# Conformer convolution accumulated in two PSUM banks, and 40 modulation row sums split between GpSimd and ScalarE

## The chip, the cores and the metric

The kernel runs on one core of a Trainium2 chip. The metric is the time of one execution on the device, in microseconds (us); lower is better. The engines are TensorE (PE, matmuls and transposes; PEld is its weight load), VectorE (DVE), ScalarE (ACT), GpSimd (POOL) and SyncE (SP, which issues most DMA transfers). Each engine works through its own queue of instructions strictly in order, and an instruction whose inputs or buffers are not ready holds up everything behind it in that queue.

## The reference

One layer of a hybrid diffusion backbone: 1024 latent tokens of width 1024 (16 rows of 64), and a prefix of 256 context tokens. All arithmetic is fp32. Cut to what matters here:

```
mx = split(silu(c) @ w_ada + b_ada, 6);  mc = split(silu(c_ctx) @ w_ada + b_ada, 6)
hx = modulate(rms_norm(x),   mx[0], mx[1])        # latent tokens
hc = modulate(rms_norm(ctx), mc[0], mc[1])        # context tokens
kc, vc, gtc = project_state_inputs(hc, w_in)      # the context gives keys, values, gates
fin_c       = mlstm_bidir_final(kc, vc, gtc)
ax, glx, qx, kx, vx, ox, gtx = project(hx, w_in)
hm = mlstm_bidir(qx, kx, vx, gtx, fin_c)          # 4 heads, chunked, both directions
u  = silu(layer_norm(dwconv31(ax * sigmoid(glx))))   # width 31 along rows of 64, 512 channels
y  = concat(u, sigmoid(ox) * head_norm(hm)) @ w_out
x  = x + mx[2] * rms_norm(y)
x  = x + mx[5] * rms_norm(conv_ffn(modulate(rms_norm(x), mx[3], mx[4])))
```

## The kernel before, in words

Channels lie on the 128 partitions, tokens along the free dimension. A matmul operand is split into a high and a low half (`hi` by a rounding copy on ScalarE, `lo = x - hi` by a subtraction on VectorE or GpSimd), and each product is three matmuls: hi·hi, hi·lo, lo·hi.

Stages, in order of time. (1) Norm and modulation of the latent tokens, and the first half of the gated projection for channel blocks j = 0 and 1. (2) `glu_evac` (L271) takes the two PSUM tiles of one block and one half of the tokens: sigmoid on ScalarE, product on VectorE (L274), which gives `u[j]`, a tile of 128 channels x 1024 tokens. Blocks j = 2 and 3 follow, one projection each. (3) `vpass(1)` multiplies ten token tiles by the value and gate weights of two heads (L556 to L558): eight latent tiles first, then two context tiles; ScalarE copies the values out (L562), VectorE the gate columns (L565). Ahead of the sixth tile the code calls `ctx_prepare`, which norms and transposes the context, scales it (L358, VectorE) and splits it into `hcT`: hi on ScalarE (L362), lo on VectorE (L363). The last two tiles of `vpass(1)` read `hcT`, so they need L362 and L363. (4) `gates` (L574 to L657), a chain of small VectorE operations and PE transposes, which needs the gate columns of all ten tiles. `vpass(0)`, the values of the other two heads, and the key and query projections run about it. (5) The four mLSTM heads; their denominators are chains of tiny VectorE operations on a tile `dn` (L813 to L818). (6) Output projection, from 460.9 us, then the FFN to the end.

Beside this runs the depthwise convolution, `conv(j)` for each of the 4 channel blocks (L276). ScalarE starts an accumulator with the middle tap and the bias (L278), and 30 `scalar_tensor_tensor` instructions on VectorE (L286, "taps") add the other taps, one after another and in place: accumulator = u shifted x weight + accumulator, over 784 to 1008 elements. The accumulator `accf` lies in two SBUF tiles of the pool `s8`, one for j = 0 and 1, one for j = 2 and 3. `hcT` takes two later tiles of the same pool. The convolutions stand in `prio(100000)`: the framework's scheduler, which fixes one order per engine when the program is built, puts such an instruction where nothing more urgent is ready by its own reckoning. The result is only read by `conv_norm`, late in the heads.

The modulation vectors `c @ w_ada` are row sums on VectorE: `mod_sum` (L228) multiplies a 128 x 1024 tile of the weights by the broadcast vector and accumulates each row's sum into one column, in one instruction. The first ones belong to stage 1. `ada_stream` issues 48 later ones: 16 for the context (`w` = 1, tiles `t`), ahead of the convolutions, and 32 for the latent tokens (`w` = 0, tiles `raw`), spread over stages 4 and 5.

GpSimd makes `lo` halves of some weights (L134, L382), a few memsets, and the small power operations of the norms (L141).

PSUM has eight banks of 512 fp32 columns: pool `mm` holds four tiles of one bank, pool `tp` four. `TP()` gives the next tile of `tp`. In the heads each chunk takes two of them, `pv` and `pc`.

Of the kernel before, what the change touches and what calls it, by code (L numbers as in the profile page):

```python
# [8 lines left out]
F32 = mybir.dt.float32  # L9
F32R = mybir.dt.float32r  # L10
AF = mybir.ActivationFunctionType
ALU = mybir.AluOpType

P = 128
# [10 lines left out]
CW = 31  # L25
W = 64
# [4 lines left out]
def hybrid_block(ctx: ExitStack, tc: tile.TileContext, x, cx, cc, small, gb, w_ada,  # L31
                 wblk, wva, wvb, w_out, w_up, w_down, out):
    nc = tc.nc
    act, dve, pool, pe, sp = nc.scalar, nc.vector, nc.gpsimd, nc.tensor, nc.sync
# [7 lines left out]
    wp = wide.enter_context(tc.tile_pool(name="wp", bufs=11))  # L42
    s8 = wide.enter_context(tc.tile_pool(name="s8", bufs=12))
    mm = wide.enter_context(tc.tile_pool(name="mm", bufs=4, space=bass.MemoryType.PSUM))
    tp = wide.enter_context(tc.tile_pool(name="tp", bufs=4, space=bass.MemoryType.PSUM))
    early = ExitStack()
    t4 = early.enter_context(tc.tile_pool(name="t4", bufs=10))

# [20 lines left out]
    def wide_tile(n, per, dt=F32):  # L69

        return Cols([S8(dt).rearrange("p (k n) -> p k n", k=per) for _ in range(n // per)])
# [10 lines left out]
    def MM():  # L82
        return mm.tile([P, 512], F32, tag="mm", name="mm")

    def TP():
        return tp.tile([P, 512], F32, tag="tp", name="tp")

    def H2(n=512):
        return sm.tile([P, 512], F32, tag="h2", name="h2", bufs=8)[:, 0:n]
# [137 lines left out]
    def mod_sum(r, s, w, ch, k):  # L227
        dve.scalar_tensor_tensor(out=r, in0=r, scalar=1.0, in1=s, op0=ALU.mult, op1=ALU.mult,  # L228
                                 accum_out=mod[:, w, ch, k:k + 1])
# [45 lines left out]

    def conv(j):  # L276
        uv = u[j].rearrange("p (r c) -> p r c", c=W)
        act.activation(out=accf[:, j], in_=u[j], func=AF.Identity, scale=conv_w[:, j, 15:16],  # L278
                       bias=conv_b[:, j:j + 1])
        for t in range(CW):  # L280
            o = t - 15
            if o == 0:
                continue
            lo, hi = max(0, -o), min(W, W - o)
            dst = accf[:, j].rearrange("p (r c) -> p r c", c=W)[:, :, lo:hi]
            dve.scalar_tensor_tensor(out=dst, in0=uv[:, :, lo + o:hi + o], scalar=conv_w[:, j, t:t + 1],  # L286
                                     in1=dst, op0=ALU.mult, op1=ALU.add)


    AB2 = const.tile([P, 2, 8], F32, name="AB2")  # L290
    Gt = {}

    def ada_stream(jobs, pl):
        for w, ch, done in jobs:
            s = ada_rows(w)
            for k in range(KT):
                r = pl()
                sp.dma_start(r, w_ada[ch * KT + k])
                mod_sum(r, s, w, ch, k)
                if done and k == KT - 1:  # L300
                    done()
                yield
# [173 lines left out]
    for j in range(2):  # L476
        u[j] = T4()
        for hf in range(2):
            glu_evac(j, hf, *ps0[j, hf])
    accf = wide_tile(4, 2)  # L480
    vw = None
    with prio(100000):
        conv(0)
# [260 lines left out]
    def mlstm_head(h):  # L744
# [38 lines left out]
        for g in range(2):  # L783
# [9 lines left out]
            for t in range(4):  # L793
                if t == 2 and pend and hn is not None:
                    yield from tails()
                c = 4 * g + t
                cs = slice(c * P, (c + 1) * P)
                pv, pc = TP(), TP()
                nv = pv[:, 0:258].rearrange("p (d n) -> p d n", d=2)
                nc_ = pc[:, 0:258].rearrange("p (d n) -> p d n", d=2)  # L800
                pl.matmul(pc[:, 0:258], qT[:, cs], Cs[c // 4][:, c % 4].rearrange("p d n -> p (d n)"),
                          start=True, stop=True)
                yield
                for d in range(2):
                    pl.matmul(nv[:, d], Dt[d][:, cs], vx[h][:, c, :], start=True, stop=True)
                    yield
                gc = gcol(0, h, c)
                gs = slice(gc, gc + 63, 62)

                dn = SM(4, "dn")  # L810
                rr, rw = dn[:, 0:2], dn[:, 2:4]
                one = lambda v: v[:, :, 128:129].rearrange("p d o -> p (d o)")
                dve.tensor_tensor(out=rr, in0=one(nc_), in1=wcol[:, gs], op=ALU.mult)  # L813
                dve.tensor_tensor(out=rr, in0=one(nv), in1=rr, op=ALU.add)
                dve.scalar_tensor_tensor(out=rw, in0=rr, scalar=-1.0, in1=rr, op0=ALU.mult, op1=ALU.max)
                dve.tensor_tensor(out=rr, in0=rw, in1=thr[:, gs], op=ALU.max)
                dve.reciprocal(out=rr, in_=rr)
                dve.tensor_tensor(out=rw, in0=rr, in1=wcol[:, gs], op=ALU.mult)  # L818
                act.mul(out=hh[:, t], in_=nv[:, 0, 0:128], mul=rr[:, 0:1])
                for src, w in ((nv[:, 1], rr[:, 1:2]), (nc_[:, 0], rw[:, 0:1]), (nc_[:, 1], rw[:, 1:2])):  # L820
                    dve.scalar_tensor_tensor(out=hh[:, t], in0=src[:, 0:128], scalar=w, in1=hh[:, t],
                                             op0=ALU.mult, op1=ALU.add)
                dve.bn_stats(out=st[:, c], in_=hh[:, t])
                dve.bn_aggr(out=mv[:, c], in_=st[:, c])
# [40 lines left out]
    uf = accf  # L865

    def conv_norm():
        for hf in range(2):
            xh = [T4().rearrange("p (t n) -> p t n", n=512) for _ in range(2)]
            mv = SM(8, "cmv").rearrange("p (t s) -> p t s", s=2)  # L870
# [616 lines left out]
```

## Time and profile before

| | |
|---|---|
| median of 3 runs | 1222.4 us (1220.09 to 1223.69) |
| profiled execution | 1219.96 us, span 1217.9 us |
| PE busy | 1146.2 us (94%) |
| DVE busy | 933.1 us (77%) |
| ACT busy | 524.0 us (43%) |
| POOL busy | 123.1 us (10%) |
| TensorE granted clock, mean | 0.986 |

The span is the time from the first to the last recorded instruction; the execution's own time is some 2 us longer. A busy share is an average over the stages. The profile cuts the span into forty slices; in those from the second to the tenth DVE is busy for 90% or more, while over the whole span it is at 77%.

### The profile page before, as it was taken

How to read it: one execution, taken by the hardware profiler on the slowest of the kernel's cores; microseconds unless marked ns; L12 is line 12 of the kernel's file. 1: busy time of each engine (PE TensorE's matmuls, PEld its weight loads, DVE VectorE, ACT ScalarE, POOL GpSimd, SP SyncE). 2: the span in 40 equal slices, each digit the busy share in tenths (PEclk: the TensorE clock that was granted, in tenths of full speed). 3: DMA queues.
4: the chain of work that ended last, by engine and by line, in shares of the span. 5: the costliest groups of instructions: out<-in, count | busy, mean ns of one | idle time of the engine just before them, and what ended most of it. 6: DMA issues, size and time to landing. Idle time of an engine off the chain costs nothing.

```text
span 1217.9 us, 14933 instructions
## 1 busy us (share of the span) xinstructions
PE 1146.2 (94%) x5463; PEld 937.5 (77%) x5463; DVE 933.1 (77%) x1702; ACT 524.0 (43%) x952; POOL 123.1 (10%) x106
## 2 busy tenths in 40 slices
PE   6999797998999999996999999999999979999997
PEld 5888787877787877874887888888887758888885
DVE  4999999999679993469757676686767755896485
ACT  6523131422666543376435334343434326454451
POOL 3624110102212100110000000000000000000010
PEclk9999999999999999998999999999999989999999
DMA  8862110531244411531313231323223158732361
GB/s 335 316 215 82 50 36 1 192 121 36 104 136 140 140 67 43 191 133 52 129 61 130 87 130 44 130 94 122 76 97 113 52 180 315 266 96 95 139 224 69
DMA packets 58991, 153.42 MB, mean 126 GB/s; under 512 B 5589, under 2 KB 5925, under 8 KB 58918
## 3 DMA queue, kind: packets, MB, share of 16 engines
q1 hardware_dynamic: 47830, 132.28, 31.5%
q10 hardware_dynamic: 11088, 20.19, 4.4%
q8 instruction: 43, 0.70, 0.2%
q14 instruction: 30, 0.25, 0.1%
HBM read 123.83 MB, written 28.61 MB: 125 GB/s over the span
## 4 chain that ended last, share of the span: by engine, by line
PE 61%; DVE 7%; ACT 1%; issue 1%; POOL 0%; DMA 0%; POOLq 0%; DVEq 0%; ACTq 0%
PE mm L1126 8%; PE mm L1128 8%; PE mm L1127 8%; PE c L1314 3%; PE c L1315 3%; PE tp L1128 3%; PE tp L1126 3%; PE tp L1127 3%; PE c L1316 3%; PE a L1316 2%; PE a L1315 2%; PE a L1314 2%; PE mm L951 2%; PE mm L952 2%; PE mm L953 2%; PE tp L508 2%
## 5 line engine op out<-in xcount | busy, mean ns | idle before, releaser
L286 DVE SCALAR_TENSOR_TENSOR s<-t,sml,s 128x864 f32<-128x864 f32 (+14 forms) x120 | 152.5, 1311 | 0.1
L150 PE MATMUL mm<-s,w 128*128 128x512 f32 (+1 forms) x320 | 127.1, 400 | 0.0
L151 PE MATMUL mm<-s,w 128*128 128x512 f32 (+1 forms) x320 | 124.9, 394 | 0.1
L1292 DVE TENSOR_TENSOR d<-d,d 128x512 fp32r<-128x512 f32 x143 | 90.3, 689 | 37.7 <-ACT d L1306 37.7
L1306 ACT ACTIVATE d<-d 128x512 fp32r<-128x512 f32 x143 | 80.4, 623 | 74.1 <-PE a L1316 27.7
L133 ACT ACTIVATE w<-raw 128x1024 fp32r<-128x1024 f32 x94 | 97.0, 1054 | 27.0 <-DMA raw<-in_w_out_dram 6.0
L1126 PE MATMUL mm<-s,w 128*128 128x512 f32 x264 | 104.8, 397 | 1.0 <-ACT h L1193 0.7
L1128 PE MATMUL mm<-s,w 128*128 128x512 f32 x264 | 104.0, 395 | 0.7 <-DVE w L134 0.7
L1127 PE MATMUL mm<-s,w 128*128 128x512 f32 x264 | 104.2, 395 | 0.0
L154 PE MATMUL mm<-s,w 128*128 128x512 f32 (+1 forms) x320 | 93.8, 402 | 0.0
L134 DVE TENSOR_TENSOR w<-raw,w 128x1024 fp32r<-128x1024 f32 x77 | 92.1, 1221 | 2.0 <-ACT w L133 1.2
L141 POOL TENSOR_TENSOR r<-yw,mhalf 128x1 f32<-128x1 f32 x16 | 12.5, 781 | 713.1 <-DVE yw L140 709.0
L1314 PE MATMUL c<-d 128*128 128x512 f32 x176 | 69.5, 395 | 8.4 <-ACT d L1306 7.6
L1126 PE MATMUL tp<-s,w 128*128 128x512 f32 x176 | 70.4, 400 | 6.1 <-ACT w L1111 6.1
L1126 PE MATMUL mm<-x,w 128*128 128x512 f32 x176 | 70.6, 401 | 1.0 <-ACT h L1184 0.7
L1128 PE MATMUL mm<-x,w 128*128 128x512 f32 x176 | 69.6, 396 | 1.9 <-DVE w L134 1.9
L151 PEld LDWEIGHTS mm<-s,w 128*128 128x128 f32 x320 | 61.3, 191 | 11.8 <-POOL s L265 0.8
L1128 PE MATMUL tp<-s,w 128*128 128x512 f32 x176 | 70.2, 399 | 0.0
L1127 PE MATMUL mm<-x,w 128*128 128x512 f32 x176 | 69.4, 394 | 0.8 <-DVE x L1051 0.8
L1127 PE MATMUL tp<-s,w 128*128 128x512 f32 x176 | 70.0, 398 | 0.0
L1178 DVE TENSOR_TENSOR h<-mm,h 128x512 f32<-128x512 f32 x22 | 15.2, 692 | 71.3 <-PE mm L1128 71.3
L150 PEld LDWEIGHTS mm<-s,w 128*128 128x128 f32 x320 | 61.3, 192 | 10.9
(284 smaller groups left out, 2788.2 us busy)
## 6 DMA issues: line engine op xcount, KB each, us to landing
raw<-in_w_up_dram SPq DMA_DIRECT2D x44, 512.0 KB, 4.6
zv<-s ACTq DMA_DIRECT2D x77, 256.0 KB, 3.0
raw<-in_w_ada_dram SPq DMA_DIRECT2D x32, 512.0 KB, 4.2
t<-in_w_ada_dram SPq DMA_DIRECT2D x28, 512.0 KB, 4.7
d<-zv SPq DMA_DIRECT2D x14, 1024.0 KB, 5.4
d<-in_w_down_dram SPq DMA_DIRECT2D x44, 256.0 KB, 6.0
raw<-in_wblk_dram SPq DMA_DIRECT2D x20, 512.0 KB, 4.5
d<-zv SPq DMA_DIRECT2D x7, 768.0 KB, 6.0
```

The source lines that it names most:

```text
L133: act.activation(out=hi, in_=raw, func=AF.Copy)
L134: (eng or pool).tensor_tensor(out=lo, in0=raw, in1=hi.bitcast(F32), op=ALU.subtract)
L150: pe.matmul(o, w[0][:, k], hi[:, k], start=(k == 0), stop=False)
L151: pe.matmul(o, w[0][:, k], lo[:, k], start=False, stop=False)
L154: pe.matmul(o, w[1][:, k], hi[:, k], start=False, stop=(k == KT - 1))
L286: dve.scalar_tensor_tensor(out=dst, in0=uv[:, :, lo + o:hi + o], scalar=conv_w[:, j, t:t + 1], in1=dst, op0=ALU.mult, op1=ALU.add)
L1126: pe.matmul(ps, w[0][:, s], b[0][:, k], start=(start and k == 0), stop=False, skip_group_check=True)
L1127: pe.matmul(ps, w[0][:, s], b[1][:, k], start=False, stop=False, skip_group_check=True)
L1128: pe.matmul(ps, w[1][:, s], b[0][:, k], start=False, stop=(k == 3), skip_group_check=True)
L1292: dve.tensor_tensor(out=o, in0=x, in1=y, op=ALU.subtract)
L1306: act.activation(out=o[:, n], in_=x, func=AF.Copy)
L1314: pe.matmul(ps, o[:, 0, s], o[:, 2], start=start, stop=False, skip_group_check=True)
```

## The change

Four things. The convolution accumulates in a new tile `cv` of two PSUM banks (the pool `tp` shrinks from four banks to two); only the last tap, now t = 16, writes `accf` in SBUF, for columns 0 to 62 of each row, and ScalarE copies column 63 (L309). There is one `cv` tile, so a convolution can start (L301) only when the one before has been read out. While no convolution is live, `TP()` hands out the halves of `cv` on two of four turns; while one is, the heads take `pc` from `mm`. Last, 40 of the 48 later row sums (8 of the 16 for the context, all 32 for the latent tokens) become a product in place on GpSimd and a row sum on ScalarE (L316, L317). Lines are renumbered: the taps L286 are L307, L274 is L294, the lo split L363 is L389, the hi split L362 is L388, the matmuls L556 to L558 are L583 to L585, L565 is L592.

```diff
-    tp = wide.enter_context(tc.tile_pool(name="tp", bufs=4, space=bass.MemoryType.PSUM))
+    tp = wide.enter_context(tc.tile_pool(name="tp", bufs=2, space=bass.MemoryType.PSUM))
+    cv = wide.enter_context(tc.tile_pool(name="cv", bufs=1, space=bass.MemoryType.PSUM))
...
+    def CV():
+
+        return cv.tile([P, 2, 512], F32, tag="cv", name="cv")
+
+    conv_live = []
+    halves_left = []
+    tp_turn = [0]
+
     def TP():
+
+        if not conv_live:
+            tp_turn[0] += 1
+            if tp_turn[0] % 4 in (3, 0):
+                if not halves_left:
+                    pair = CV()
+                    halves_left.extend((pair[:, 1], pair[:, 0]))
+                return halves_left.pop()
         return tp.tile([P, 512], F32, tag="tp", name="tp")
+
+    def HP():
+        return MM() if conv_live else TP()
...
     def conv(j):
         uv = u[j].rearrange("p (r c) -> p r c", c=W)
-        act.activation(out=accf[:, j], in_=u[j], func=AF.Identity, scale=conv_w[:, j, 15:16],
-                       bias=conv_b[:, j:j + 1])
-        for t in range(CW):
+        pair = CV().rearrange("p h n -> p (h n)")
+        pv = pair.rearrange("p (r c) -> p r c", c=W)
+        fv = accf[:, j].rearrange("p (r c) -> p r c", c=W)
+        act.activation(out=pair, in_=u[j], func=AF.Identity, scale=conv_w[:, j, 15:16], bias=conv_b[:, j:j + 1])
+
+        for t in (*range(15), *range(17, CW), 16):
             o = t - 15
-            if o == 0:
-                continue
             lo, hi = max(0, -o), min(W, W - o)
-            dst = accf[:, j].rearrange("p (r c) -> p r c", c=W)[:, :, lo:hi]
+            dst = (fv if o == 1 else pv)[:, :, lo:hi]
             dve.scalar_tensor_tensor(out=dst, in0=uv[:, :, lo + o:hi + o], scalar=conv_w[:, j, t:t + 1],
-                                     in1=dst, op0=ALU.mult, op1=ALU.add)
+                                     in1=pv[:, :, lo:hi], op0=ALU.mult, op1=ALU.add)
+        act.copy(out=fv[:, :, W - 1:W], in_=pv[:, :, W - 1:W])
...
+    def mod_sum_pool(r, s, w, ch, k):
+        pool.tensor_tensor(out=r, in0=r, in1=s, op=ALU.mult)
+        act.activation(out=r, in_=r, func=AF.Identity, accum_out=mod[:, w, ch, k:k + 1])
...
-                mod_sum(r, s, w, ch, k)
+                (mod_sum if w and k % 2 == 0 else mod_sum_pool)(r, s, w, ch, k)
...
     accf = wide_tile(4, 2)
+    conv_live.append(True)
...
-                pv, pc = TP(), TP()
+                pv, pc = TP(), HP()
...
     def conv_norm():
+        conv_live.clear()
```

The order that the scheduler gives the engines moves with it. In VectorE's queue before, the four lo splits of the context (L363; `s_1280` is its hi tile, `s_1281` its lo tile) stand here, among the taps:

```order
L286 SCALAR_TENSOR_TENSOR s_739<-t_725,sml,s_739 128x16x56
L565 COPY h_1111<-mm 128x2x2x4
L358 TENSOR_SCALAR h_1287<-tp,AB 128x256 x2
L358 TENSOR_SCALAR h_1297<-tp,AB 128x256 x2
L363 TENSOR_TENSOR s_1281<-h_1287,s_1280 128x512
L358 TENSOR_SCALAR h_1307<-tp,AB 128x256
L363 TENSOR_TENSOR s_1281<-h_1297,s_1280 128x512
L358 TENSOR_SCALAR h_1307<-tp,AB 128x256
L358 TENSOR_SCALAR h_1317<-tp,AB 128x256 x2
L363 TENSOR_TENSOR s_1281<-h_1307,s_1280 128x512
```

There 43 of the 120 taps stand ahead of the first lo split. In VectorE's queue after the change, the same four splits (now L389, of `s_1295` into `s_1296`) stand behind the last tap of conv(2); `s_747` is the half of `accf` for j = 2 and 3, and `t_984` is u[3]:

```order
L307 SCALAR_TENSOR_TENSOR cv<-t_826,sml,cv 128x16x50
L307 SCALAR_TENSOR_TENSOR cv<-t_826,sml,cv 128x16x49
L307 SCALAR_TENSOR_TENSOR s_747<-t_826,sml,cv 128x16x63
L389 TENSOR_TENSOR s_1296<-h_1302,s_1295 128x512
L389 TENSOR_TENSOR s_1296<-h_1312,s_1295 128x512
L389 TENSOR_TENSOR s_1296<-h_1322,s_1295 128x512
L389 TENSOR_TENSOR s_1296<-h_1332,s_1295 128x512
L307 SCALAR_TENSOR_TENSOR cv<-t_984,sml,cv 128x16x49
```

So 90 taps stand ahead of the first lo split in place of 43, all those of conv(0), conv(1) and conv(2). In ScalarE's queue after the change, the hi splits (L388) stand behind the end of conv(1) (the copy L309 into `s_746`, the half of `accf` for j = 0 and 1) and the start of conv(2) (L301 from `t_826`, u[2]):

```order
L309 COPY s_746<-cv 128x16
L301 ACTIVATE cv<-t_826,sml 128x1024
L388 ACTIVATE s_1295<-h_1302 128x512
L388 ACTIVATE s_1295<-h_1312 128x512
L388 ACTIVATE s_1295<-h_1322 128x512
L388 ACTIVATE s_1295<-h_1332 128x512
L309 COPY s_747<-cv 128x16
```

Before, copies of values (L562) stood directly ahead of the first hi split (L362) in that queue; the last start of a convolution (L278) stood four rows above it, and waited for its u[3] alone. In PE's queue after the change, the matmuls of the first context tile come directly behind those of the eighth latent tile (`s_116`, `s_118`); `s_111` is a tile of `vpass(0)`:

```order
L584 MATMUL mm<-w,s_116 128x272
L585 MATMUL mm<-w,s_118 128x272
L583 MATMUL mm<-w,s_1295 128x272
L584 MATMUL mm<-w,s_1295 128x272
L583 MATMUL mm<-w,s_1295 128x272
L584 MATMUL mm<-w,s_1295 128x272
L583 MATMUL mm<-w,s_111 128x256
L585 MATMUL mm<-w,s_1296 128x272
L583 MATMUL mm<-w,s_1295 128x272
```

One matmul of `vpass(0)` stands among those of the context tiles; the rest of `vpass(0)`, and all that comes later, stands behind them, as it did before the change. In GpSimd's queue the eight products for the context stand ahead of the lo halves of the value weights (L408, which was L382):

```order
L285 TENSOR_TENSOR s_114<-h_625,s_112 128x512
L316 TENSOR_TENSOR t_676<-t_676,t_670 128x1024
L316 TENSOR_TENSOR t_683<-t_683,t_670 128x1024
L316 TENSOR_TENSOR t_690<-t_690,t_670 128x1024
L316 TENSOR_TENSOR t_697<-t_697,t_670 128x1024
L316 TENSOR_TENSOR t_704<-t_704,t_670 128x1024
L154 TENSOR_TENSOR w<-raw,w 128x1024
L316 TENSOR_TENSOR t_711<-t_711,t_670 128x1024
L316 TENSOR_TENSOR t_718<-t_718,t_670 128x1024
L316 TENSOR_TENSOR t_725<-t_725,t_670 128x1024
L154 TENSOR_TENSOR w<-raw,w 128x1024 x2
L408 TENSOR_TENSOR w<-raw,w 128x816 x2
```

Before, the subtraction L265 (L285 now) was followed at once by the weight subtractions L134 (L154 now) and L382.

## Rows read from the trace of the kernel before

**Rows 1.** Page: each engine's busy time, share of the span, instructions.

```profile
PE 1146.2 (94%) x5463; PEld 937.5 (77%) x5463; DVE 933.1 (77%) x1702; ACT 524.0 (43%) x952; POOL 123.1 (10%) x106
```

**Rows 2.** Windows; columns: window, length, busy (instructions) of PE, PEld, DVE, ACT, POOL.

```profile
core 0: us, PE busy (x) PEld busy (x) DVE busy (x) ACT busy (x) POOL busy (x), PEclk, DMA share, GB/s
71.10:123.80 52.70, 52.70 (x229) 42.60 (x228) 52.56 (x61) 15.66 (x22) 16.25 (x11) 1.00 0.46 158
...
166.30:221.90 55.60, 46.74 (x325) 42.41 (x324) 55.38 (x85) 13.59 (x35) 7.26 (x6) 0.97 0.12 40
221.90:310.00 88.10, 81.42 (x435) 67.97 (x434) 86.61 (x181) 25.23 (x66) 18.11 (x8) 0.98 0.34 113
310.00:460.90 150.90, 143.65 (x795) 118.55 (x794) 127.59 (x470) 88.89 (x213) 25.85 (x19) 1.00 0.35 118
460.90:1217.90 757.00, 727.81 (x3148) 584.26 (x3146) 517.50 (x768) 330.07 (x531) 16.89 (x24) 0.99 0.35 123
```

**Rows 3.** Windows again, of the stretch from the first lo split to the gates' end.

```profile
158.50:221.70 63.20, 53.37 (x368) 48.16 (x367) 62.98 (x98) 16.89 (x46) 8.51 (x6) 0.97 0.10 34
```

**Rows 4.** Instructions of the taps: durations in ns (min/median/max), first and last start.

```profile
L286 DVE SCALAR_TENSOR_TENSOR s<-t,sml,s x120: 1001/1158/3342, 94.8 to 304.9; 128x784 f32<-128x784 f32 x8, 128x800 f32<-128x800 f32 x8, 128x816 f32<-128x816 f32 x8, 128x832 f32<-128x832 f32 x8
```

**Rows 5.** Timeline of VectorE, 75 to 145 us: start, time, line, operation, count.

```profile
75.97 3.45 DVE L228 SCALAR_TENSOR_TENSOR t<-t,t 128x1024 f32<-128x1024 f32 x1
...
83.19 1.22 DVE L228 SCALAR_TENSOR_TENSOR t<-t,t 128x1024 f32<-128x1024 f32 x1
...
94.82 8.98 DVE L286 SCALAR_TENSOR_TENSOR s<-t,sml,s 128x784 f32<-128x784 f32 x3
103.73 0.68 DVE L274 TENSOR_TENSOR t<-mm,h 128x512 f32<-128x512 f32 x1
...
117.20 10.95 DVE L286 SCALAR_TENSOR_TENSOR s<-t,sml,s 128x896 f32<-128x896 f32 x10
...
141.64 2.84 DVE L347 TENSOR_SCALAR t<-t,rsc 128x1024 f32<-128x1024 f32 x1 [0.60 <-POOL rsc L141]
...
144.49 0.74 DVE L347 TENSOR_SCALAR t<-t,rsc 128x1024 f32<-128x1024 f32 x1
```

**Rows 6.** Timeline of GpSimd, 75 to 145 us.

```profile
75.95 2.40 POOL L134 TENSOR_TENSOR w<-raw,w 128x1024 fp32r<-128x1024 f32 x1 [4.42 <-PE mm L151]
94.80 5.50 POOL L134 TENSOR_TENSOR w<-raw,w 128x1024 fp32r<-128x1024 f32 x2 [16.45 <-ACT w L133]
100.26 7.47 POOL L382 TENSOR_TENSOR w<-raw,w 128x816 fp32r<-128x816 f32 x3
...
141.58 2.35 POOL L382 TENSOR_TENSOR w<-raw,w 128x1024 fp32r<-128x1024 f32 x1
```

**Rows 7.** Instructions by line, as in Rows 4: sums, splits, scales, copies, start.

```profile
L228 DVE SCALAR_TENSOR_TENSOR t<-t,t x16: 1212/1219/3453, 71.1 to 92.4; 128x1024 f32<-128x1024 f32 x16
L358 DVE TENSOR_SCALAR h<-tp,AB x8: 535/540/544, 156.7 to 161.1; 128x256 f32<-128x256 f32 x8
L363 DVE TENSOR_TENSOR s<-h,s x4: 684/684/693, 158.5 to 162.3; 128x512 fp32r<-128x512 f32 x4
L565 DVE COPY h<-mm x10: 163/176/183, 144.4 to 176.9; 128x16 f32<-128x16 f32 x10
L278 ACT ACTIVATE s<-t,sml x4: 1243/1246/1247, 92.5 to 138.7; 128x1024 f32<-128x1024 f32 x4
```

**Rows 8.** Waits of PE, 120 to 225 us: total us, times, longest.

```profile
PE tp L508 <- DVE gsc L617: 4.9, 1, 4.9
...
PE tp L508 <- DVE ccol L601: 1.9, 1, 1.9
```

**Rows 9.** Groups of VectorE instructions from 460 us: busy us, mean ns.

```profile
L1178 DVE TENSOR_TENSOR h<-mm,h 128x512 f32<-128x512 f32 x22 | 15.2, 692 | 71.3 <-PE mm L1128 71.3
L1157 DVE TENSOR_TENSOR s<-h,h 128x512 f32<-128x512 f32 x22 | 15.1, 689 | 1.5 <-ACT h L1141 1.5
```

**Rows 10.** Instructions on the tile `dn` in the heads, as in Rows 4.

```profile
L815 DVE SCALAR_TENSOR_TENSOR dn<-dn x32: 139/152/2215, 272.5 to 449.9; 128x2 f32<-128x2 f32 x32
L816 DVE TENSOR_TENSOR dn<-dn,thr x32: 125/154/2355, 272.7 to 450.8; 128x2 f32<-128x2 f32 x32
```

**Rows 11.** Waits of PE, 221 to 461 us, as in Rows 8.

```profile
PE tp L508 <- DVE h L821: 6.2, 6, 1.6
PE tp L508 <- ACT h L720: 2.3, 1, 2.3
```

## The prediction

> **What bounds the kernel now.** I began with the page: PE is busy for 94% of the span, VectorE for 77%, GpSimd for 10% [rows 1]. Such a share hides stages, so I went on to the windows. From 71 to 310 us VectorE is busy for all but a few tenths to 1.5 us of each stretch; from 71 to 123.8 PE is too [rows 2]. After that PE idles: 55.6 - 46.7 = 8.9 us to 221.9, 88.1 - 81.4 = 6.7 us to 310, 150.9 - 143.7 = 7.3 us in the heads, so 22.9 us in all [rows 2]. This is the most that a less loaded VectorE could give back before the output projection starts at 460.9. Behind that stand 757 us with 727.8 us of PE work [rows 2], which the change does not touch. PE is therefore the bound, and VectorE counts only where its queue hands something late to PE. Then I read which hand-over that is about the change, from the two orders, and timed it in the trace: before, the first lo split of the context starts at 158.5, and PE takes the context tiles up at once [rows 7]. From there to the gates' end at 221.7 PE works 53.4 of 63.2 us [rows 3].
>
> **The change, part by part.**
>
> *The new wait.* The lo splits L389 stand in VectorE's queue behind all 90 taps of conv(0), conv(1) and conv(2), in place of 43. The context matmuls need them, and in PE's queue nearly all of `vpass(0)`, the key and query projections and the heads stand behind these matmuls. So PE finishes the eight latent tiles and stops until VectorE has done conv(2). The prediction is, above all, the time at which that happens. I add up VectorE's queue from 71.1 us, where the later sums start:
>
> - 8 sums left for the context at 1.15 us from start to start (an unhindered one lasts 1.22 and the next begins 0.07 us before its end [rows 5]): 9.2.
> - 8 products of `glu_evac` at 0.60 (0.68 less the same overlap [rows 5]): 4.8.
> - 90 taps. Ten of about 920 elements on average, beside no GpSimd work, last 10.95 us [rows 5]; the 30 taps of one convolution average 896 elements, so 1.06 each, 31.9 for a convolution, 95.6 for three.
> - The small ones: 8 scales at 0.54, 8 gate copies at 0.18, two L347 at 0.74 [rows 5, 7]: 7.2, estimated.
>
> That is 116.8 us, and would put the first lo split at 187.9 if VectorE never waited. To this come:
>
> - *GpSimd against the eight sums.* A sum that coincided with a GpSimd subtraction took 3.45 us in place of 1.22, and three taps beside five such subtractions took 8.98 us in place of about 2.9 [rows 5, 6]; a product that reads PSUM was not held up (0.68 at 103.73, in the middle of L382 [rows 5, 6]). An instruction with two SBUF inputs is thus held by a whole GpSimd operation. Eight products of some 2.35 us [rows 6] now run just where the eight sums stand: between 0 (they miss each other) and 8 x 2.35 + one L154 = 22. The taps lost (8.98 - 2.9)/5, or about 1.2 us, to each GpSimd operation, the sum 2.2; I take 2.0 for each of 8: 16.
> - *Taps beside GpSimd.* With their accumulator in PSUM they have one SBUF input, like L274, so I add nothing; in the 95.6 above they are already unhindered. The relief from the 3342 ns of the worst tap [rows 4] is in that price.
> - *PSUM in place of SBUF.* Reading one input from PSUM costs VectorE the same (692 against 689 ns for 512 elements [rows 9]). VectorE writing into PSUM in place is not in the trace. Nothing excludes that it is slower; from below the bound is 0, and I take 0, since the reading side shows 0. A tap that took twice its streaming time is a rival below.
> - *Hand-over between convolutions.* With one `cv`, conv(1) and conv(2) each wait for the copy of the last column and a start of 1.24 us on ScalarE [rows 7]; with 0.4 for the copy, estimated between nothing and that start, 2 x 1.65 = 3.3.
> - *L347 held by a GpSimd subtraction*, as before (2.84 against 0.74 [rows 5]): 2. *Scales waiting for transposes* out of two `tp` buffers: 1, from 0 to 3 (one L347 held longer).
>
> Together 187.9 + 16 + 3.3 + 2 + 1 = 210 us, against 158.5 before: **the context tiles come 51.7 us later**, and PE stands still for about 50 us before them.
>
> [...]
>
> *What is given back.* After the splits only conv(3) is left, and no sums. From the first lo split to the gates' end VectorE had 63.0 us of work, most of it taps; now it has about 31.9 + 2.7 and the small operations, some 44. PE's 53.4 us [rows 3] become the floor, plus what the gates' own chain makes PE wait (4.9 + 1.9 for `gsc` and `ccol` [rows 8]), of which I leave 2.8. So 56.2 in place of 63.2: -7, bounds 0 and -9.8. From 221.9 to 310 there are no taps left; of 6.7 us of idle time I take -5, bounds 0 and -6.7.
>
> *The 32 products in stages 4 and 5.* Each frees VectorE of 1.15 us, and holds its two-input SBUF operations for up to 2.35. On `dn` this already shows: a median of 0.15 us, and a maximum of 2.2 and 2.4 [rows 10], and PE waits 6.2 us for what ends that chain [rows 11]. One against the other I take +2, from -3 to +15. The row sums, about 1.25 us each on ScalarE as L278 [rows 7], make 40 us over more than 230, where ScalarE is busy for 114 of 239 [rows 2]; hidden by that gap. Were it gone, PE's wait for ScalarE in the heads (2.3 [rows 11]) would grow.
>
> *The rest.* PSUM keeps its eight banks. `pc` from `mm` and halves of `cv` from `TP()` change waits by less than I can read: 0.
>
> **Sum:** 51.7 - 7 - 5 + 2 = +41.7 us. The profiled execution took 1219.96 us (span 1217.9), so it becomes about 1262; the median lies 2.4 us above that execution, so 1222.4 + 41.7, or **1264 us**.
>
> **The rivals.**
>
> 1. *VectorE is early and PE catches up.* The sums and products miss each other (no 16), and all idle time to 310 is given back: 51.7 - 16 - 9.8 - 6.7 + 2 = +21, so 1243. For it: GpSimd's products are cheap to place since VectorE has 8 products of `glu_evac` from PSUM in between. Against: the gates are a chain that PE must wait for in part. Chance 16%.
> 2. *The heads pay.* Every second product holds a `dn` operation, and the small power operations of the norms queue behind products on GpSimd: +15 in place of +2, and nothing given back to 310: 51.7 + 15 = +67, so 1289. For it: the maxima on `dn`. Against: VectorE loses 32 x 1.15 = 37 us of sums. Chance 13%.
> 3. *Taps in place in PSUM are slow.* At twice the streaming time, 896 elements cost 0.93 us more: 90 x 0.93 = 84 before the splits, 28 after, most of that beside PE work: +41.7 + 84 + 5, so about 1353. Only the silence of the trace speaks for it. Chance 5%.
> 4. *Faster or no loss: cheap taps.* If taps in PSUM took clearly less than in SBUF, the splits would come early. Break-even with 22.9 us of idle time all given back needs the first lo split by 181.4, so 90 taps in 181.4 - 71.1 - 21.2 - 3.3 = 85.8 us, 0.95 us each in place of 1.06, and not one held sum. At 0.85 us the split comes at 172 and the time is about 1213. Against: equal prices for PSUM and SBUF [rows 9]. Chance 4%. That the splits don't wait at all would need another order than the one printed; VectorE and PE take their queues in order.
>
> **How the numbers follow.** The forecast (+28 to +58, its own range 1250 to 1280) gets 62%, rival 1 16%, rival 2 13%, rival 3 5%, rival 4 4%. The terms' own bounds, from no held sums to 22 us and a slow `tp`, move the forecast by -16 to +8, and the give-back by -5 to +12. The range reaches to rival 1 and rival 2: 1236 to 1290; outside remain rivals 3 and 4 and the tails of 1 and 2, some 17%. A measurement of this kernel can tell a change of about 0.3%, 3.7 us, from none: faster comes only from rival 4 (3%), the same from its edge (2%), slower 95%.
>
> **What the profile after would show.** Right: one stretch of some 50 us in which PE stands still, ended by L389 through `s_1296`, with the first L389 near 210 us; 116 taps into `cv` with hardly any above 1.3 us; sums L248 near 3.4 us beside L316 from 71 to 100 us; a shorter way from L389 to the gates' end, about 56 us; heads of nearly the same length, and about 757 us from the output projection on. Wrong: a first lo split before 190 or after 222; PE waiting for ScalarE or GpSimd in the heads for more than some 10 us more than now; taps near 2 us; or PE busy with `vpass(0)` during conv(2).

## The result, and the profile after

The changed kernel takes 1340.7 us (median; 1336.7 to 1341.8), the kernel before 1222.4 us: the ratio is 1.096, 95% interval 1.094 to 1.099. The prediction was 1264 us, with a range to 1290. The direction and the place of the first loss were right; a stretch that I had priced at -3 us cost 64.6.

The page of the changed kernel, each engine's busy time, to be held against [rows 1]:

```profile
PE 1172.3 (88%) x5463; PEld 954.7 (72%) x5463; DVE 946.0 (71%) x1622; ACT 569.0 (43%) x1036; POOL 214.4 (16%) x146
```

PE has 26 us more busy time for the same 5463 matmuls, VectorE 13 us more for 80 instructions fewer, and GpSimd 91 us more. To see where the time went I cut both traces at the same three events: the first lo split of the context, the end of the gates (the copy into `dec`), and the last matmul of the output projection's first matmul line. These are the rows of the three lines in the changed kernel (durations in ns, first and last start), and the projection's row of the kernel before, which was not shown above:

```profile
L389 DVE TENSOR_TENSOR s<-h,s x4: 684/686/687, 220.6 to 222.4; 128x512 fp32r<-128x512 f32 x4
```

```profile
L684 DVE COPY dec<-tp x1: 282/282/282, 272.3 to 272.3; 128x128 f32<-128x128 f32 x1
```

```profile
L979 PE MATMUL mm<-w,s x128: 387/396/990, 538.9 to 649.6; 128*128 128x512 f32 x128
```

```profile
L951 PE MATMUL mm<-w,s x128: 388/394/584, 434.0 to 534.4; 128*128 128x512 f32 x128
```

| stretch | before | after | difference | predicted |
|---|---|---|---|---|
| to the first lo split | 158.5 | 220.6 | +62.1 | +51.7 |
| from there to the gates' end | 63.2 | 51.7 | -11.5 | -7 |
| from there to the output projection's end | 312.7 | 377.3 | +64.6 | -3 |
| from there to the end | 683.5 | 685.3 | +1.8 | 0 |

The first column follows from [rows 3] and the row just shown; I call the third stretch the heads. Windows of the changed kernel at these events (columns as in [rows 2]):

```profile
71.10:166.30 95.20, 84.26 (x449) 72.45 (x447) 88.74 (x94) 30.81 (x58) 43.90 (x21) 0.95 0.30 100
166.30:220.60 54.30, 1.49 (x5) 1.18 (x5) 51.23 (x45) 3.50 (x6) 0.00 (x0) 0.50 0.00 0
220.60:272.30 51.70, 47.76 (x340) 44.52 (x341) 47.62 (x73) 16.54 (x42) 12.34 (x8) 0.96 0.09 25
272.30:649.60 377.30, 323.84 (x1578) 261.73 (x1577) 223.48 (x621) 178.10 (x398) 115.85 (x70) 0.94 0.30 102
649.60:1334.90 685.30, 656.33 (x2820) 526.42 (x2818) 482.65 (x703) 300.62 (x473) 9.19 (x10) 0.98 0.35 122
```

From 166 to 220.6 us PE does 1.5 us of work while VectorE is full: that is the stop that the order announced. In the heads it is the other way round: VectorE is busy for only 223 of 377 us, PE for 324, and nothing is full. So there PE waits for the end of chains, and not for an engine that has too much to do. The waits of PE (total us, times, longest), against [rows 8, 11]:

```profile
PE mm L585 <- DVE s L389: 34.3, 1, 34.3
PE mm L583 <- ACT s L388: 22.7, 1, 22.7
PE tp L535 <- DVE h L848: 13.9, 6, 5.5
PE cv L535 <- DVE h L848: 11.2, 5, 3.7
```

The first two rows are one stop of 57 us, the hi splits behind conv(1) and then the lo splits behind conv(2). The next two lie in the heads: PE waits for a PSUM tile that L848, the last reader of a chunk's products, has not yet let go. The same wait was 6.2 us before [rows 11].

### The profile page after: what moved, and what is told of

Read it like the earlier page. It is cut to its first block, busy times and chain, and to the rows that moved or that the text cites. A ratio compares the mean times of both kernels' runs of the same rounds, so it can differ in the third digit from the quotient of the medians.

```text
span 1334.9 us, 14928 instructions
## 1 busy us (share of the span) xinstructions
PE 1172.3 (88%) x5463; PEld 954.7 (72%) x5463; DVE 946.0 (71%) x1622; ACT 569.0 (43%) x1036; POOL 214.4 (16%) x146
## 4 chain that ended last, share of the span: by engine, by line
PE 56%; DVE 12%; ACT 2%; issue 2%; POOL 2%; DMA 1%; DVEq 0%; POOLq 0%; ACTq 0%
PE mm L1154 7%; PE mm L1156 7%; PE mm L1155 7%; PE c L1342 3%; PE c L1343 3%; PE c L1344 3%; PE a L1343 2%; PE a L1344 2%; PE a L1342 2%; PE mm L979 2%; PE mm L981 2%; PE mm L980 2%; PE cv L535 2%; PE tp L535 2%; DVE h L859 1%
## 5 line engine op out<-in xcount | busy, mean ns | idle before, releaser
L170 PE MATMUL mm<-s,w 128*128 128x512 f32 (+1 forms) x320 | 133.6, 421 | 7.5 <-ACT h L293 7.5
L307 DVE SCALAR_TENSOR_TENSOR cv<-t,sml,cv 128x784 f32<-128x784 f32 (+14 forms) x116 | 133.3, 1149 | 7.0 <-ACT cv L301 3.9
L171 PE MATMUL mm<-s,w 128*128 128x512 f32 (+1 forms) x320 | 128.5, 405 | 1.1 <-POOL s L285 1.1
L174 PE MATMUL mm<-s,w 128*128 128x512 f32 (+1 forms) x320 | 95.7, 414 | 0.0
L154 DVE TENSOR_TENSOR w<-raw,w 128x1024 fp32r<-128x1024 f32 x77 | 93.9, 1245 | 2.3 <-ACT w L153 1.2
L316 POOL TENSOR_TENSOR raw<-raw,G 128x1024 f32<-128x1024 f32 x32 | 75.7, 2377 | 52.6 <-DMA raw<-in_w_ada_dram 46.7
L1342 PE MATMUL c<-d 128*128 128x512 f32 x176 | 69.9, 398 | 8.4 <-ACT d L1334 7.6
L170 PEld LDWEIGHTS mm<-s,w 128*128 128x128 f32 x320 | 63.3, 198 | 19.3 <-ACT h L293 8.0
L585 PE MATMUL mm<-w,s 128*128 128x272 f32 (+1 forms) x160 | 46.2, 290 | 34.3 <-DVE s L389 34.3
L171 PEld LDWEIGHTS mm<-s,w 128*128 128x128 f32 x320 | 63.6, 199 | 12.9 <-POOL s L285 1.9
L1343 PE MATMUL c<-d 128*128 128x512 f32 x176 | 69.6, 396 | 0.0
L1344 PE MATMUL c<-d 128*128 128x512 f32 x176 | 69.5, 395 | 0.0
```

The lines of the kernel that those rows point to most:

```text
L154: (eng or pool).tensor_tensor(out=lo, in0=raw, in1=hi.bitcast(F32), op=ALU.subtract)
L170: pe.matmul(o, w[0][:, k], hi[:, k], start=(k == 0), stop=False)
L171: pe.matmul(o, w[0][:, k], lo[:, k], start=False, stop=False)
L174: pe.matmul(o, w[1][:, k], hi[:, k], start=False, stop=(k == KT - 1))
L1342: pe.matmul(ps, o[:, 0, s], o[:, 2], start=start, stop=False, skip_group_check=True)
L1343: pe.matmul(ps, o[:, 0, s], o[:, 3], start=False, stop=False, skip_group_check=True)
```

## The experiments

Twelve kernels ran, each timed in turn with the kernel before. Ratios are to that kernel, with 95% intervals. Theory A was that the heads' loss is the price of the split sums, theory B that it is the price of the banks.

**1. The changed kernel with all sums on VectorE.**

```diff
-                (mod_sum if w and k % 2 == 0 else mod_sum_pool)(r, s, w, ch, k)
+                mod_sum(r, s, w, ch, k)
```

> The changed kernel with all 48 later sums back on VectorE; convolution and banks as changed. Of the 117 us that the change cost, 62 lie ahead of the first lo split, 60 in the heads, 6 behind them, and 11 come back in the gates. Theory A (the heads' 60 us are the price of the split sums: GpSimd waits for transfers, ScalarE waits for GpSimd, dn operations are held): first lo split near 211 us, heads as long as before, about 1270 us. Theory B (the heads' 60 us are the price of the banks: two tp tiles and pairs): heads as long as after, about 1328 us.

Measured: 1306.8 us, ratio 1.069 (1.066 to 1.071). First lo split at 221.8, heads 347.8 us. Both theories miss: of the heads' 64.6 us, 35 stay and 30 go. The split did not come forward either (221.8 us, and 220.6 with the products): VectorE has eight more sums to do, and GpSimd's weight subtractions hold others of its instructions (two sums took 3.41 us, one L373 2.80; in the kernel before 3.45 and, as L347, 2.84 [rows 5, 6]).

**2. The sums alone, on the kernel before.**

```diff
-                mod_sum(r, s, w, ch, k)
+                (mod_sum if w and k % 2 == 0 else mod_sum_pool)(r, s, w, ch, k)
```

> The kernel before with only the 40 sums split between GpSimd and ScalarE; convolution in SBUF, four tp tiles. The order has 45 taps ahead of the first lo split. Theory A: heads 60 us longer, about 1280 us. Theory B: heads within 10 us of before, about 1228 us.

Measured: 1279.4 us, ratio 1.047 (1.045 to 1.049), with heads 46 us longer, the first lo split 8.5 us later and the gates 5 us longer. The time is theory A's, but theory A put 60 us into the heads.

**3. The lo splits freed.** The accumulator tile for j = 2 and 3 is first written by conv(2)'s last tap in the changed kernel, and the `hcT` tiles, which come later from the same pool, stand behind that write. One memset gives the tile an early first write.

```diff
     conv_live.append(True)
+    pool.memset(accf[:, 2, 0:1], 0.0)
```

> The changed kernel with one memset of a column of the accumulator tile for j = 2 and 3 right behind its allocation, which moves the lo splits in VectorE's order from behind 90 taps to behind 39. If the late splits are what costs the time to the gates, PE's 57 us stop at the context tiles goes, and about 50 us of the 117 come back: 1290 us, with heads still some 60 us longer than before. If the stop only moves elsewhere (a later convolution holds the single accumulator, or conv_norm waits), 1320 us or more.

Measured: 1281.1 us, ratio 1.048 (1.047 to 1.050). The splits start earlier than in the kernel before:

```profile
L389 DVE TENSOR_TENSOR s<-h,s x4: 679/681/691, 155.0 to 158.8; 128x512 fp32r<-128x512 f32 x4
```

60 us of the 118 came back, the gates end at 215.5 us, and the heads are as long as after (376 us). So the late splits are what costs, as the first answer had it, and one memset of one column is worth half of the loss.

**4. The banks alone, on the kernel before.** Pools, `TP`, `HP` and the flag of the change; `conv` as before, in SBUF, and all sums on VectorE.

```diff
-    tp = wide.enter_context(tc.tile_pool(name="tp", bufs=4, space=bass.MemoryType.PSUM))
+    tp = wide.enter_context(tc.tile_pool(name="tp", bufs=2, space=bass.MemoryType.PSUM))
+    cv = wide.enter_context(tc.tile_pool(name="cv", bufs=1, space=bass.MemoryType.PSUM))
...
-                pv, pc = TP(), TP()
+                pv, pc = TP(), HP()
```

> The kernel before with only the bank scheme of the change (two tp tiles, cv pairs handed out by turns, pc from mm while the flag is set); the convolution accumulates in SBUF as before, all sums on VectorE. Theory A: within 8 us of before, about 1226 us. Theory B: heads some 60 us longer, about 1280 us.

Measured: 1267.3 us, ratio 1.037 (1.034 to 1.039), heads 42 us longer. So A and B both hold, each for a part; what was to be settled next was the mechanism in each. PE waits 16.5 us here for L846, the last reader of a chunk's products, where it waited 6.2 before [rows 11]:

```profile
PE tp L533 <- DVE h L846: 7.0, 5, 2.1
PE cv L533 <- DVE h L846: 5.5, 4, 1.7
PE mm L170 <- DVE h L846: 4.0, 1, 4.0
```

**5. GpSimd's products without anything that uses them.** VectorE keeps its 48 sums, ScalarE gets none.

```diff
                 mod_sum(r, s, w, ch, k)
+                if not (w and k % 2 == 0):
+                    pool.tensor_tensor(out=r, in0=r, in1=s, op=ALU.mult)
```

> The kernel before with all 48 sums on VectorE as before; behind 40 of them GpSimd multiplies the same tile once more in place, a product that nothing reads. ScalarE gets no row sums. The split sums alone cost 57 us (38 of them between the gates' end and the output projection). Theory A1 (GpSimd's products hold VectorE's two-input SBUF operations): the cost stays, 1265 us or more, since VectorE keeps the sums as well. Theory A2 (ScalarE, in order, stands at a row sum until GpSimd has its product, 57 us of waiting in that stage): the cost goes, about 1230 us.

Measured: 1301.6 us, ratio 1.065 (1.064 to 1.067): 79 us for 40 idle products; A1 had said 1265 or more.

**6. The row sums without GpSimd.**

```diff
+    def mod_sum_act(r, s, w, ch, k):
+        act.activation(out=r, in_=r, func=AF.Identity, accum_out=mod[:, w, ch, k:k + 1])
...
-                mod_sum(r, s, w, ch, k)
+                (mod_sum if w and k % 2 == 0 else mod_sum_act)(r, s, w, ch, k)
```

> The kernel before with 40 of the 48 sums as a row sum on ScalarE alone; the product with the modulation input is left out, so GpSimd does nothing more than before and VectorE has 40 sums fewer. Theory A1 (holds by GpSimd): faster than before or the same, 1212 to 1225 us. Theory A2 (ScalarE in order behind late tiles): still 20 us or more slower, 1242 us or more, since the row sums now wait for the transfers themselves.

Measured: 1214.9 us, ratio 0.994 (0.993 to 0.996), as A1 had it. This kernel leaves out the product with the modulation input. The kernel of experiment 2 differs from this one by its 40 products on GpSimd alone, and takes 64.5 us more. The heads' windows (columns as in [rows 2]) of the kernel before, of experiment 2, of experiment 5, and of experiment 6:

```profile
221.70:534.40 312.70, 298.77 (x1557) 245.88 (x1556) 249.15 (x716) 143.73 (x337) 51.65 (x40) 0.99 0.36 120
```

```profile
235.40:594.50 359.10, 316.96 (x1553) 259.39 (x1553) 265.15 (x651) 179.03 (x399) 124.61 (x70) 0.94 0.30 105
```

```profile
241.80:615.80 374.00, 314.13 (x1556) 255.67 (x1555) 303.27 (x716) 144.93 (x337) 129.84 (x70) 0.94 0.29 100
```

```profile
218.30:528.20 309.90, 298.75 (x1549) 247.21 (x1549) 219.23 (x651) 178.63 (x399) 44.84 (x40) 0.99 0.35 121
```

Read VectorE's column, the third busy time. Between experiments 2 and 6 it has the same 651 instructions and 265.2 against 219.2 us; between experiment 5 and the kernel before the same 716, and 303.3 against 249.2. These 46 and 54 us are time in which VectorE's instructions were held, 1.5 to 1.8 us to each of the 30 products of this stretch. ScalarE is equally loaded in experiments 2 and 6 (179.0 and 178.6), so its load is not the cause. In experiment 2, from 235 to 513 us, it waited long for GpSimd's products, and GpSimd for the tiles:

```profile
ACT raw L295 <- POOL raw L294: 57.3, 17, 7.3
```

```profile
POOL raw L294 <- DMA raw<-in_w_ada_dram: 53.0, 15, 15.0
```

These rows looked like the culprit (theory A2). The loss does not need them: in experiment 5, without any row sum on ScalarE, it stayed, and in experiment 6 the row sums waited for transfers and cost nothing. Whether they add to the loss of experiment 2 was not measured by itself. What grows with the products is PE's wait in the heads for the last reader of a chunk's products, here in experiments 2 and 6:

```profile
PE tp L512 <- DVE h L825: 20.3, 8, 4.7
```

```profile
PE tp L511 <- DVE h L824: 2.7, 3, 2.0
```

Which instructions are held shows in experiment 5 on `dn`, against [rows 10]:

```profile
L817 DVE SCALAR_TENSOR_TENSOR dn<-dn x32: 139/152/2351, 312.5 to 522.4; 128x2 f32<-128x2 f32 x32
L818 DVE TENSOR_TENSOR dn<-dn,thr x32: 122/152/2384, 312.7 to 526.1; 128x2 f32<-128x2 f32 x32
L819 DVE RECIPROCAL dn<-dn x32: 125/155/166, 313.9 to 529.2; 128x2 f32<-128x2 f32 x32
L820 DVE TENSOR_TENSOR dn<-dn,wcol x32: 133/152/2326, 314.1 to 530.0; 128x2 f32<-128x2 f32 x32
```

Operations with two SBUF inputs reach 2.3 to 2.4 us, even for two elements, which is as long as a whole product (2.33 to 2.46 us for the 32 on `raw` in the changed kernel); the reciprocal between them, with one input, is not held in any of its 32. But one tensor input is no protection in general: a `TENSOR_SCALAR` from SBUF to SBUF, the last step of the heads' norm, is held as well. Here it is in experiment 5, and in the kernel before:

```profile
L834 DVE TENSOR_SCALAR h<-h,mv,hrs x32: 312/339/2399, 367.2 to 538.3; 128x128 f32<-128x128 f32 x32
```

```profile
L832 DVE TENSOR_SCALAR h<-h,mv,hrs x32: 316/340/349, 323.1 to 460.6; 128x128 f32<-128x128 f32 x32
```

One point stays open: in experiments 2 and 5 a `raw` tile also comes free later than in experiment 6, and how much of the loss this adds was not separated. In the heads of experiment 2 no wait of PE ends with a weight half made from such a tile; in those of experiment 5 one of 7.4 us does.

**7. The two banks as single tiles**, on the kernel of experiment 4.

```diff
-    cv = wide.enter_context(tc.tile_pool(name="cv", bufs=1, space=bass.MemoryType.PSUM))
+    cv = wide.enter_context(tc.tile_pool(name="cv", bufs=2, space=bass.MemoryType.PSUM))
...
-        return cv.tile([P, 2, 512], F32, tag="cv", name="cv")
+        return cv.tile([P, 512], F32, tag="cv", name="cv")
...
-                if not halves_left:
-                    pair = CV()
-                    halves_left.extend((pair[:, 1], pair[:, 0]))
-                return halves_left.pop()
+                return CV()
```

> The bank scheme alone on the kernel before (45 us slower), but with the two cv banks as two tiles of one bank each, which come free one by one in place of as a pair. Convolution in SBUF, all sums on VectorE. Ahead of the end of conv_norm the scheme alone costs 15 us, behind it 21 us, to which comes the stretch ahead of the gates' end. If the pair is what costs behind conv_norm: 21 to 30 us come back, 1240 us. If it is that only two tp tiles stand while the convolution is live, and the later stage only follows: within 8 us of 1267.

Measured: 1239.1 us, ratio 1.013 (1.012 to 1.015): 28 of the 45 us were the pair, the first answer. A new pair is handed out only when both halves of the one before are free, so the slower chunk holds both banks.

**8. The taps on one accumulator in SBUF.** The changed kernel, with a tile `chain` in SBUF for the two banks (and one tile less in pool `wp`).

```diff
-        pair = CV().rearrange("p h n -> p (h n)")
+        pair = chain
```

> The changed kernel with the accumulator of the convolution in one SBUF tile in place of the two banks (pool wp one tile smaller to make room); taps still one after another on one accumulator. In the changed kernel the 29 taps from 185 us run from start to start in 1.186 us on average, where before independent neighbours took 1.06 for the same mean length. If PSUM costs the 0.13 us: 1.06 here beside no GpSimd work. If a tap must wait for the one before on the same accumulator: 1.17 to 1.19 here too.

Measured: 1347.5 us, ratio 1.103 (1.100 to 1.105). Timelines of VectorE where GpSimd does nothing, of the changed kernel and of this one: 29 taps of one convolution, and the last.

```profile
185.00 34.40 DVE L307 SCALAR_TENSOR_TENSOR cv<-t,sml,cv 128x784 f32<-128x784 f32 x29 [1.55 <-ACT cv L301]
219.43 1.26 DVE L307 SCALAR_TENSOR_TENSOR s<-t,sml,cv 128x1008 f32<-128x1008 f32 x1
```

```profile
194.79 34.29 DVE L310 SCALAR_TENSOR_TENSOR chain<-t,sml,chain 128x784 f32<-128x784 f32 x29 [1.37 <-ACT chain L304]
229.12 1.27 DVE L310 SCALAR_TENSOR_TENSOR s<-t,sml,chain 128x1008 f32<-128x1008 f32 x1
```

34.40 and 34.29 us: PSUM costs 4 ns a tap. What costs is the chain. Before, neighbours in the queue mostly belonged to different convolutions, and ten taps of 920 elements took 10.95 us [rows 5]; here each tap reads what the one before it wrote.

**9. Both repairs at once:** experiment 1 with the memset of experiment 3.

> The changed kernel with both repairs at once: the memset that frees the lo splits (37 taps ahead of them), and all 48 sums on VectorE. What stays of the change is the convolution in two banks and the bank scheme. If the shares simply add: 1341 - 60 - 34 = 1247 us. If the bank scheme sets the time whatever else is repaired: as the scheme alone, 1267 us.

Measured: 1265.9 us, ratio 1.036 (1.034 to 1.038): the second answer. The shares don't add; with the splits freed, putting the sums back gives 15 us and not 34, and what is left is the time of the bank scheme alone (experiment 4).

**10. Single banks, always four.** Experiment 7 with the flag never set.

```diff
-    conv_live.append(True)
```

> The bank scheme on the kernel before as two single banks, and the flag of a live convolution never set, so that four banks always stand for TP in turn. The scheme alone costs 45 us, with single banks 17. If those 17 are the stage in which two tp tiles must do: 1222 to 1228 us. If they come from the turns or the order itself: 1235 us or more.

Measured: 1229.2 us, ratio 1.0065 (1.005 to 1.008), just outside the first answer. 10 of the 17 us were the stage in which `TP()` has two tiles and `pc` comes from `mm`; the other 7 stay with two pools taken in fixed turns in place of one of four.

**11. GpSimd's weight halves on VectorE,** the theory of the holds turned round on the kernel before.

```diff
-        return split_blk(raws[0]), split_blk(raws[1])
+        return split_blk(raws[0], dve), split_blk(raws[1], dve)
...
-            pool.tensor_tensor(out=lo[:, 0:c], in0=r[:, 0:c], in1=hi[:, 0:c].bitcast(F32), op=ALU.subtract)
+            dve.tensor_tensor(out=lo[:, 0:c], in0=r[:, 0:c], in1=hi[:, 0:c].bitcast(F32), op=ALU.subtract)
...
-            ahead[order[n]] = load_blk(order[n])
+            ahead[order[n]] = load_blk(order[n], dve)
```

> The kernel before with the lo halves of the later weights (L134 of the pairs and blocks from 71 us on, and L382) moved from GpSimd to VectorE, 1.2 us each there in place of some 2.5 on GpSimd; some 20 instructions. If a GpSimd operation costs VectorE about what it lasts, by holding its two-input SBUF operations: the same or faster, 1212 to 1224 us. If holds are rarer than that: VectorE, full from 71 to 310 us, gets some 20 us more to do, 1230 us or more.

Measured: 1217.5 us, ratio 0.9965 (0.9953 to 0.9976), the first answer and the only kernel here that does all the work and is faster than the one before. Windows of this kernel, and of the kernel before where [rows 2] have no such window, and an operation on `dn`:

```profile
71.10:221.90 150.80, 148.06 (x895) 130.70 (x894) 148.86 (x219) 46.61 (x103) 2.56 (x8) 1.00 0.31 107
221.90:310.00 88.10, 81.97 (x441) 68.23 (x439) 79.47 (x193) 24.48 (x52) 2.74 (x5) 0.96 0.21 69
310.00:534.00 224.00, 210.83 (x1030) 171.33 (x1031) 158.11 (x521) 112.14 (x264) 20.42 (x25) 0.95 0.35 119
```

```profile
71.10:221.90 150.80, 133.12 (x805) 117.11 (x804) 149.84 (x196) 38.28 (x82) 28.74 (x19) 0.99 0.22 76
...
310.00:534.00 224.00, 216.75 (x1121) 177.39 (x1120) 162.11 (x534) 117.89 (x272) 33.41 (x33) 1.00 0.36 122
```

```profile
L816 DVE TENSOR_TENSOR dn<-dn,thr x32: 127/152/161, 250.5 to 449.3; 128x2 f32<-128x2 f32 x32
```

With 23 instructions more up to 221.9 us VectorE is busy for no longer than before, PE idles for 2.7 us there in place of 17.7, and nothing on `dn` is held. Of these 15 us little arrives: up to 534 us PE idles for 19.3 us in place of 13.9, and its busy time from 71.1 to 534 us is 440.9 in place of 431.3 us for five matmuls more, at a granted clock of 0.95 in place of 1.00 in the last window. 5.4 and 9.6 us make up the lead; this profiled execution ends 2 us earlier, the median 5.

**12. Only the halves ahead of the gates on VectorE.** Experiment 11 without its last edit.

```diff
-            ahead[order[n]] = load_blk(order[n], dve)
+            ahead[order[n]] = load_blk(order[n])
```

> As e11, but only the lo halves of the block pair and of the value weights move to VectorE, those ahead of the gates; the twelve blocks of the heads stay on GpSimd. In e11 the gates ended 17 us earlier and the heads took 15 us of it back. If the heads' share is the price of twelve subtractions more on VectorE there: 1206 to 1213 us. If the heads give the lead back anyway, since their own chains set the pace: 1215 to 1222 us.

Measured: 1223.9 us, ratio 1.0025 (1.001 to 1.004): no gain, and just above even the second answer. The windows at the same bounds:

```profile
71.10:221.90 150.80, 145.91 (x878) 129.43 (x877) 149.37 (x211) 43.05 (x90) 14.71 (x12) 0.99 0.28 95
221.90:310.00 88.10, 80.05 (x437) 66.37 (x436) 81.07 (x182) 27.09 (x63) 12.59 (x8) 1.00 0.25 84
310.00:534.00 224.00, 207.17 (x1033) 168.55 (x1032) 160.27 (x521) 110.10 (x261) 30.78 (x29) 0.97 0.35 119
```

A lead of 12.8 us at 221.9 goes into idle time of PE, 8.1 and 16.8 us in place of 6.7 and 7.3. Which chain of the heads sets this pace is not settled.

## Why the prediction was right or wrong

*The new wait: right.* PE stood still for 57 us before the context tiles, released by L388 and L389, as read from the order; freed, 60 us came back (experiment 3). The split came at 220.6 us in place of 210. The held sums were sized well, some 15 us for 16: of the eight, five lasted 3.35 to 3.42 us in place of 1.22, and two tiny operations behind them were held for 2.1 and 2.3. One reading under that term was loose: only three to four of the five subtractions ran beside the three taps at 94.82 [rows 5, 6], so each cost those taps nearer 1.7 than 1.2 us. The rows:

```profile
74.54 3.40 DVE L248 SCALAR_TENSOR_TENSOR t<-t,t 128x1024 f32<-128x1024 f32 x1
...
88.01 2.09 DVE L254 TENSOR_TENSOR AB<-mod,b 128x8 f32<-128x8 f32 x1
90.13 2.31 DVE L255 TENSOR_TENSOR AB<-AB,sml 128x8 f32<-128x8 f32 x1
```

*The price of a tap: mis-sized.* I took 1.06 us, from neighbours that did not depend on each other; a tap of nearly the same mean length (892 elements) that follows its own accumulator takes 34.40/29 = 1.19. Added up over VectorE's timeline, the 90 taps ahead of the split took about 105 us in place of 95.6, which is most of the 10.6 us by which the split was late. That taps with their accumulator in PSUM are no longer held was right: none of the 116 lasted over 1.28 us.

```profile
L307 DVE SCALAR_TENSOR_TENSOR cv<-t,sml,cv x116: 1019/1156/1273, 102.2 to 265.8; 128x784 f32<-128x784 f32 x8, 128x800 f32<-128x800 f32 x8, 128x816 f32<-128x816 f32 x8, 128x832 f32<-128x832 f32 x8
```

*PSUM at the price of SBUF: right.* Experiment 8 measured 4 ns a tap. Rival 3, slow taps in PSUM, is out, though its 1353 us lie near the result. Its 0.93 us for 896 elements agree with 1.04 ns an element, an estimate from 1219 ns for 1024 elements [rows 7] and 689 for 512 [rows 9].

*Given back to the gates' end: the right sign, too small.* It was -11.5 for -7, outside the bounds of 0 and -9.8. I had taken PE's 53.4 us as the floor, and PE had less to do there: 340 matmuls in 47.8 us, against 368 [rows 3].

*"One against the other I take +2": the step that failed.* I set the 1.15 us that VectorE saves on a sum against the time that a product holds it, as if both were throughput. Experiments 6 and 2 measure them apart: taking the sums off VectorE gains 7.5 us, the products cost 64.5. In the changed kernel the split sums are 30 of the heads' 64.6 us (experiment 1), and the -5 that I had given back to 310 us did not come. VectorE was not full in the heads; there it is a link in a chain, from a chunk's products over `dn` to the PSUM tile that PE needs next, and a hold of 2.3 us on a 0.15 us operation goes into that chain: with the products PE's wait at its end is 20.3 us in place of 2.7. The maxima in [rows 10] showed such holds, and rival 2 named them, but at +15.

*"`pc` from `mm` and halves of `cv` from `TP()`: 0": failed as well.* In the changed kernel the heads keep 35 us of loss with no split sums (experiment 1). The bank scheme alone costs 45 us (experiment 4), 28 of them for the pair (experiment 7), 10 for the stage with two tiles and 7 for the turns (experiment 10). PE's waits for a tile in the heads, 6.2 us [rows 11], were a sign that four tiles were already short.

*The clock, left out of the sum.* In the heads PE was granted 0.94 on average, against 0.99 before, and 0.50 in the stop (the window from 166.3 to 220.6 us). PE's busy time in the heads went from 298.8 to 323.8 us. The 21 matmuls more are some 4 us of that, at 298.8/1557 us each, an estimate; the rest, some 21 of the heads' 64.6 us, is the same work done more slowly, besides the idle time, which rose from 13.9 to 53.5 us. What lowered the clock is not shown by itself; in the windows of the experiments it was 0.94 where PE idled for 42 or 60 us (experiments 2 and 5) and 0.99 where it idled for 11 (experiment 6).

So the 118 us are: late splits, sums and banks, worth 60, 57 and 45 us when each is removed or made alone. The last two lie largely over each other: together, with the splits freed, they cost 59 us (experiment 3).

## What to carry to other kernels

Work moved to GpSimd was not off VectorE here, where VectorE has operations with two SBUF inputs, or a `TENSOR_SCALAR` from SBUF to SBUF: with medians of 0.15 and 0.34 us, they reached 2.4 us beside products of 2.7 us on average (experiment 5). What that costs depends on who waits for the short ones, not on busy shares: 40 idle products cost 79 us. A tile's first write places it in the order: when a change moves that write behind a long chain, later tiles of the same pool go with it (60 us here, experiment 3), and the order shows this before anything runs. PSUM tiles that are allocated as a pair come free as a pair; where PE already waited for tiles, the pair cost 28 us (experiment 7).

## What the runs showed of the hardware that was not expected

A VectorE instruction that reads what the one directly before it wrote started later here than one that does not: a tap of about 890 elements after 1.19 us, in SBUF and in PSUM alike (34.29 and 34.40 us for 29), against 1.06, an estimate from ten taps of 920 elements in 10.95 us [rows 5]. Taps of one convolution also share their `u`; that this is not needed for the delay shows in two tiny operations of the kernel before. The second reads the `AB` that the first wrote and starts 0.20 us after it; the sum behind it, which needs neither, starts after 0.08, at 83.19 [rows 5].

```profile
82.91 0.17 DVE L234 TENSOR_TENSOR AB<-mod,b 128x8 f32<-128x8 f32 x1
83.11 0.17 DVE L235 TENSOR_TENSOR AB<-AB,sml 128x8 f32<-128x8 f32 x1
```

By the two prices of a tap, two convolutions interleaved run 11% faster than one after the other, an estimate; no run interleaves them in PSUM.

Forty products that nothing reads, on an engine that was busy for 10% of the span, cost 79 us, 2.0 us each, where a product itself lasted 2.7 us on average (107 us for 40 in experiment 5).
